# Second feed-forward of a transformer layer: five even features first on one token half alone, with their partial sums kept in DRAM

## The chip, the cores and the metric

The kernel runs on one core of a Trainium2 chip. The metric is the device time of one execution in microseconds (us), as the median of several runs. The engines are named as in the profile: PE multiplies matrices (PEld is its loading of weights), DVE, ACT and POOL do elementwise work, SP issues DMA transfers.

## What is computed

One layer works on 1024 latent tokens (a context of 256 tokens takes part in the mixing) with model width 1024 and feed-forward width 2816. The change lies in the second feed-forward alone, in the last line of this cut:

```python
def swiglu(h, w1, w3, w2):
    return (jax.nn.silu(h @ w1) * (h @ w3)) @ w2
...
x = x + 0.5 * m_l[2][:, None, :] * swiglu(modulate(rms_norm(x, norm1_w[i]), m_l[0], m_l[1]), ...)
y_l, y_c = token_mixing(modulate(rms_norm(x, norm2_w[i]), m_l[3], m_l[4]), ...)
x = x + m_l[5][:, None, :] * y_l
x = x + 0.5 * m_l[8][:, None, :] * swiglu(modulate(rms_norm(x, norm3_w[i]), m_l[6], m_l[7]), ...)
```

All of it is float32. m_l are nine modulation vectors, computed from c by a matrix product with ada_w.

## The kernel before, in words

**Precision.** A float32 operand is split into a high and a low part (`split`: ACT writes hi, DVE writes lo = x - hi). A product of two such operands is three matmuls, hi·hi, hi·lo, lo·hi (`mm3`, L424 to L428; the names hh and hl are the parts of h, whi and wlo those of a weight). One block product here is a block of 512 model rows by one feature block of 128 by 512 tokens: four k blocks of three matmuls, so 12 matmuls of 512 columns.

**The feed-forward in blocks.** The 2816 features are 22 blocks of 128 ("features" 0 to 21), taken in pairs (f, f+1); the tokens are two halves of 512 (0 and 1); the model rows are two halves. The product of a pair of features with both token halves is a 2 by 2 by 2 block product, which `chain` does with seven block products in place of eight (Winograd's form), from sums of weights (`seven_w`) and sums of h, called T1 to T4. A pair so has 7 products for w1 and 7 for w3, 168 matmuls. The result of w1 goes through silu on ACT (`c_silu`, L738), that of w3 is multiplied on DVE (`c_mul`, L743). When the four blocks g of a pair are there, `g_out` forms four differences on DVE (L751) and stores seven blocks to the DRAM tensor gd (L752), from which the last product with w2 reads them later.

**The opening.** T1 to T4 need the normed h of both halves, and the norm of half 1 is made only while PE has started. Therefore `first2` does features 0 and 1 without the seven-product form, on half 0 first (192 matmuls), while DVE and ACT finish the norm of half 1: `norm_t` makes for each of its k blocks nt (the scaled x), hh, hl and the raw sums of T1 and T2 (tiles t2h, t2l, t3h), all told at L147, since they come from the recorded steps of the mixing phase before. In that norm PE does two groups of eight small matmuls, psb<-ones,nacc and psb<-ndiag,ones. `HELD` puts the second of them behind a chosen matmul of the first product. Then `hidden` runs the pairs from 2 on: chain for w1, the sums of w2 (`w2_sums`, three loads by L792), chain for w3, and now and then a step of a modulation vector (L537, L538).

**What sets the order.** Every engine runs its instructions in the order in which the scheduler put them and stands still at one whose inputs are not ready. This is also so for SP, which issues all these transfers: a load behind a store that waits for DVE is issued after it. Loads of weights and their splits are pulled ahead by a priority (`WPRI`). Buffers: 6 raw weight tiles (`NR`), 6 split weights (`NH`), 19 tiles s of 128 by 512 (`ns`).

## Time and profile before

| | |
|---|---|
| median of 3 runs | 2084.39 us (2083.61 to 2087.27) |
| the profiled execution | 2088.82 us, of which the span 2087.0 us |
| PE clock granted, mean | 0.998 |
| PE busy | 2071.6 us (99% of the span) |
| DVE busy | 1471.9 us (71%) |
| ACT busy | 973.3 us (47%) |
| first product of the second feed-forward | starts at 1432.81 us |

The profile has a page and answers to queries of the trace. A row of the timeline reads: start, duration of one or of the whole group, engine, line, operation, output <- inputs, shape, and in brackets how long the engine had been idle and who released it. Rows of the waits read: engine and line that waited, for whom, us in total, times, longest. A row of windows has the stretch, then for each engine busy time and count, the PE clock granted, the share of the DMA engines in use and GB/s. A DMA row ends with its size and the us from issue to landing. Matmuls are pipelined, so that the time of one is read from the distance of starts.

### The profile page before, as it was taken

What the parts mean: (1) busy time and instruction counts of PE and PEld (TensorE: products, weight loads), DVE (VectorE), ACT (ScalarE), POOL (GpSimd) and SP (SyncE); (2) the same over time, 40 slices, a digit from 0 to 9 for tenths busy, and PEclk for the clock granted to TensorE, in tenths of its full rate; (3) what the DMA queues carried; (4) which work ended last, traced back from release to release, by engine and by line L of the source; (5) the groups of instructions that cost most, each with busy time, mean ns of one, the idle gap of its engine ahead of it and who ended that gap; (6) DMA issues with size and microseconds to landing.
All of it is one profiled execution on the core that took longest, in us unless ns stands there. A gap on an engine that the chain in (4) does not pass through costs nothing.

```text
span 2087.0 us, 34162 instructions
## 1 busy us (share of the span) xinstructions
PE 2071.6 (99%) x12352; PEld 1763.0 (84%) x12352; DVE 1471.9 (71%) x2660; ACT 973.3 (47%) x1818; POOL 199.3 (10%) x195
## 2 busy tenths in 40 slices
PE   9999999999999999999999999999999999999998
PEld 6888888888889999998788988888888888888888
DVE  6889999666776445765577478767776666765586
ACT  5433433435544445566475246444434344344553
POOL 0000000000015665001021001000000000010000
PEclk9999999999999999999999999999999999999999
DMA  9277667449886553674233233242344444477774
GB/s 348 84 241 237 232 217 256 149 165 371 277 289 222 181 183 115 195 219 129 76 108 98 79 91 105 90 162 81 112 156 147 144 163 157 151 235 229 218 237 151
DMA packets 201082, 370.58 MB, mean 178 GB/s; under 512 B 23249, under 2 KB 35921, under 8 KB 200785
## 3 DMA queue, kind: packets, MB, share of 16 engines
q1 hardware_dynamic: 200768, 368.33, 53.7%
q8 instruction: 97, 1.59, 0.3%
q14 instruction: 73, 0.59, 0.1%
q10 hardware_dynamic: 144, 0.07, 0.0%
HBM read 292.68 MB, written 67.24 MB: 172 GB/s over the span
## 4 chain that ended last, share of the span: by engine, by line
PE 77%; DVE 10%; DMA 8%; issue 3%; ACT 1%; SPq 0%; DVEq 0%; POOLq 0%; ACTq 0%
PE psa L147 18%; PE psa L426 10%; PE psa L428 10%; PE psa L427 10%; PE psb L147 9%; PE psb L427 7%; PE psb L428 7%; PE psb L426 7%; DVE junk L523 2%; DVE wlo L422 2%; DMA raw<-in_w 2%; DMA raw<-sd 2%; DVE hl L422 1%; DMA raw<-gd 1%; DMA hl<-sd 1%
## 5 line engine op out<-in xcount | busy, mean ns | idle before, releaser
L421 ACT ACTIVATE whi<-raw 128x512 fp32r<-128x512 f32 x371 | 233.9, 631 | 502.7 <-issue 160.6
L422 DVE TENSOR_TENSOR wlo<-raw,whi 128x512 fp32r<-128x512 f32 x371 | 254.1, 687 | 178.0 <-ACT whi L421 175.6
L426 PE MATMUL psa<-hh,whi 128*128 128x512 f32 x684 | 267.0, 390 | 1.2 <-ACT s L738 0.6
L428 PE MATMUL psa<-hh,wlo 128*128 128x512 f32 x684 | 266.3, 389 | 0.0
L427 PE MATMUL psa<-hl,whi 128*128 128x512 f32 x684 | 266.2, 389 | 0.0
L427 PE MATMUL psb<-hl,whi 128*128 128x512 f32 x568 | 221.6, 390 | 0.5 <-DVE hl L422 0.3
L428 PE MATMUL psb<-hh,wlo 128*128 128x512 f32 x568 | 221.3, 390 | 0.2 <-DVE wlo L422 0.2
L426 PE MATMUL psb<-hh,whi 128*128 128x512 f32 x568 | 221.1, 389 | 0.0
L426 PEld LDWEIGHTS psa<-hh,whi 128*128 128x128 f32 x684 | 128.4, 188 | 28.9 <-ACT s L711 1.7
L147 DVE TENSOR_TENSOR wlo<-raw,whi 128x512 fp32r<-128x512 f32 (+1 forms) x140 | 88.5, 647 | 90.8 <-ACT whi L147 80.1
L147 PE MATMUL psa<-hl,whi 128*128 128x512 f32 x384 | 152.5, 397 | 0.0
L147 PE MATMUL psa<-hh,whi 128*128 128x512 f32 x384 | 152.3, 397 | 0.0
L147 PE MATMUL psa<-hh,wlo 128*128 128x512 f32 x384 | 152.2, 396 | 0.0
L428 PEld LDWEIGHTS psa<-hh,wlo 128*128 128x128 f32 x684 | 128.4, 188 | 26.6
L427 PEld LDWEIGHTS psa<-hl,whi 128*128 128x128 f32 x684 | 128.5, 188 | 26.3
L422 POOL TENSOR_TENSOR hl<-s,hh 128x512 fp32r<-128x512 f32 x88 | 132.4, 1530 | 145.2 <-DVE hl L422 81.1
L147 ACT ACTIVATE whi<-raw 128x512 fp32r<-128x512 f32 (+1 forms) x140 | 82.5, 599 | 119.7 <-PE psa L147 94.1
L427 PEld LDWEIGHTS psb<-hl,whi 128*128 128x128 f32 x568 | 106.6, 188 | 24.7 <-DVE hl L422 2.7
L428 PEld LDWEIGHTS psb<-hh,wlo 128*128 128x128 f32 x568 | 106.6, 188 | 23.1 <-DVE wlo L422 1.2
L426 PEld LDWEIGHTS psb<-hh,whi 128*128 128x128 f32 x568 | 106.6, 188 | 22.2
L428 PE MATMUL psa<-hh,hl 128*128 128x256 f32 x392 | 111.1, 284 | 0.0
L426 PE MATMUL psa<-hh,hh 128*128 128x256 f32 x392 | 111.1, 283 | 0.0
(443 smaller groups left out, 4820.4 us busy)
## 6 DMA issues: line engine op xcount, KB each, us to landing
raw<-in_w SPq DMA_DIRECT2D x242, 256.0 KB, 3.3
s<-in_w SPq DMA_DIRECT2D x198, 256.0 KB, 3.7
gd<-s SPq DMA_DIRECT2D x154, 256.0 KB, 2.8
ada<-in_adaT SPq DMA_DIRECT2D x60, 512.0 KB, 4.6
raw<-gd SPq DMA_DIRECT2D x91, 256.0 KB, 3.5
sd<-s SPq DMA_DIRECT2D x44, 256.0 KB, 2.7
raw<-sd SPq DMA_DIRECT2D x44, 256.0 KB, 3.2
hh<-in_w SPq DMA_DIRECT2D x44, 256.0 KB, 4.0
```

Source lines behind the costliest of these rows:

```text
L147: self.rec.add(self.eng, lambda: f(*map(get, a), **{x: get(v) for x, v in k.items()}), outs, ins, name, a, k)
L421: nc.scalar.activation(hi, src, AF.Copy)
L422: (eng or nc.vector).tensor_tensor(out=lo, in0=src, in1=hi.bitcast(F32), op=ALU.subtract)
L426: mm(ps, wa[0], xa[0], start=start, stop=False, skip_group_check=more)
L427: mm(ps, wa[0], xa[1], start=False, stop=False, skip_group_check=more)
L428: return mm(ps, wa[1], xa[0], start=False, stop=stop, skip_group_check=more)
L523: nc.vector.tensor_tensor_reduce(out=self.junk, in0=t, in1=self.cs[s], scale=1.0, scalar=self.col("ada_b")[:, j:j + 1], op0=ALU.mult, op1= ...
```

## The change

The features 0, 2, 4, 6 and 8 are now treated in two steps.

`part(f)` takes the place of `first2`. It works on feature f and token half 0 alone. For w1 and w3 it does the first block product (12 matmuls each) into a PSUM bank; ACT copies the bank to a tile (L750), and a DMA stores the tile to a new DRAM tensor c1d (L751). Then the second product is added in the same bank, which finishes feature f on half 0: silu, multiplication, and a store of that g to gd (L755). This is 48 matmuls for each of the five parts. The splits of T1 and T2 stand between the parts 2 and 4, the raw sums of T3 and T4 between the parts 6 and 8, and their splits behind part 8.

`hidden(0, ..., 10)` then takes all pairs. The pairs 0 to 8 go through `rest`: of the seven products of each weight, the first (the saved one) and the second (feature f on half 0) are left out, which leaves five (W6, W5, W7, W3, W4), 120 matmuls for the pair. The saved sum is loaded from c1d (L776), copied by ACT into the bank (L794), and W6 accumulates on it. For w3 the saved g is loaded from gd as well (L779), and `g_out` doesn't store it again. The pairs 10 to 20 go through `chain` as before. The norm of half 1 makes no hh and hl for its first four k blocks, and the number HELD is 3 in place of 6.

```diff
 def norm_t ...
-            t = self.norm_k(tg, k, a, b, rb, pool)
+            t = self.scr(pool, "nt")
+            self.norm_a1(tg, k, a, rb, t)
...
+    def part(self, f):
+        ws = [self.load_halves(w[f]) for w in (self.w1, self.w3)]
+        ps = self.psA(), self.psB()
+        mms = []
+        for i in range(2):
+            for k in range(4):
+                mms.append(self.mm3(ps[i], self.wslice(ws[i], k), self.h[0][k], k == 0, k == 3))
+            t = self.stile()
+            self.nc.scalar.copy(t, ps[i])
+            self.nc.sync.dma_start(self.c1d[i, f // 2], t)
+        for i in range(2):
+            self.prod4(ws[i][1], self.h[0][4:], ps[i], False)
+            (self.c_mul if i else self.c_silu)(f, 0, ps[i], True)
+        self.nc.sync.dma_start(self.gd[1, f // 2], self.g[f, 0])
+        self.g[f, 0] = None
+        return mms
...
+    def rest(self, w, f, out, bank):
+        nc, i = self.nc, int(w is self.w3)
+        with self.tc.high_priority(offset=WPRI):
+            c1 = self.stile()
+            nc.sync.dma_start(c1, self.c1d[i, f // 2])
+            if i:
+                self.g[f, 0] = self.stile()
+                nc.sync.dma_start(self.g[f, 0], self.gd[1, f // 2])
+                self.again.add(f)
+            w6, w5, w7, w3, w4 = self.five_w(w, f)
...
+        a, b = bank(), bank()
+        nc.scalar.copy(a, c1)
+        self.prod4(w6, t2, a, False)
+        u2 = keep(a)
+        self.prod4(w5, t1, b, True)
+        c5 = keep(b)
+        self.prod4(w7, t3, a, False)
+        u3 = keep(a)
+        out(f + 1, 1, plus(c5, u3, c5))
+        self.prod4(w3, self.h[1][4:], b, False)
+        out(f, 1, plus(u2, b, u2))
+        self.prod4(w4, t4, a, False)
+        out(f + 1, 0, a, True)
...
-        put(1, b11), put(2, b21), put(3, b22)
+        if f not in self.again:
+            put(1, b11)
+        put(2, b21), put(3, b22)
...
-            self.chain(self.w1, f, self.c_silu, self.psA)
+            chain = self.rest if f < parts else self.chain
+            chain(self.w1, f, self.c_silu, self.psA)
...
+        mms = self.part(0)
+        tc.add_manual_dep(rec.diags[-4].ins, mms[HELD].ins.name, SCHED, reason="order")
+        self.part(2)
         for i, raw in enumerate((self.t1r, self.tr)):
             for k in range(4):
                 self.t_split(tp, i, k, raw[k])
-        raw = self.first2(tp, rec.diags[-4])
-        late = (None for _ in self.mods_half(f2, (8,)))
+        self.part(4)
+        self.part(6)
+        raw = [self.t34_raw(k) for k in range(4)]
+        self.part(8)
...
-        self.hidden(2, lambda: next(late, None))
+        late = (None for _ in self.mods_half(f2, (8,)))
+        self.hidden(0, lambda: next(late, None), False, 10)
...
-HELD = 6
+HELD = 3
```

Where the instructions now stand is shown at three places. Rows of the listing have the line, the operation and output <- inputs, with the number of each tile.

First place, ACT in the opening. The tiles t1h, t2h are hi parts of T1 and T2, hh_3173 is of the last k block of half 1, whi_15981 of a weight of part 4; psa_15785 and psb_15786 are the banks with the first products of part 0. Of the changed kernel:

```order
L422 ACTIVATE whi_15981<-raw_15979 128x512
L147 ACTIVATE hh_3173_15752<-nt_15748,mod_87 128x512
L422 ACTIVATE t1h_3243_15941<-t2l_3194_15750 128x512
L422 ACTIVATE t2h_3247_15949<-t3h_3096_15421 128x512
L422 ACTIVATE t2h_3251_15957<-t3h_3098_15458 128x512
L750 COPY s_15799<-psa_15785 128x512
L750 COPY s_15814<-psb_15786 128x512
```

The copies of part 0's first products stand behind the whole norm of half 1 and the hi parts of T1 and T2; by the listing of PE, 72 matmuls (the first products of the parts 0, 2 and 4) stand ahead of part 0's second product.

Second place, SP's queue between w3 of pair 2 and w1 of pair 4. The tiles s_16611 to s_16750 are blocks g of pair 2 and their differences, raw_17008 to raw_17012 weights of pair 6, s_16753 a piece for a modulation vector, s_16756 the saved sum for w1 of pair 4. Of the changed kernel:

```order
L665 DMA raw_17008<-in_w 128x512
L665 DMA raw_17010<-in_w 128x512
L823 DMA gd<-s_16611 128x512
L823 DMA gd<-s_16742 128x512
L823 DMA gd<-s_16745 128x512
L823 DMA gd<-s_16553 128x512
L823 DMA gd<-s_16750 128x512
L538 DMA s_16753<-in_adaT 128x512
L776 DMA s_16756<-c1d 128x512
L665 DMA raw_17012<-in_w 128x512
```

A seam between two pairs in the kernel before has these rows (s_16439 to s_16447 are blocks g and differences, the raw tiles weights that are used after a further weight set):

```order
L752 DMA gd<-s_16439 128x512
L752 DMA gd<-s_16281 128x512
L752 DMA gd<-s_16442 128x512
L752 DMA gd<-s_16222 128x512
L663 DMA raw_16770<-in_w 128x512
L752 DMA gd<-s_16447 128x512
L663 DMA raw_16772<-in_w 128x512
```

The load of the saved sum is new behind the pair's last stores; before, only loads of later weights stood there.

Third place, SP's queue between w1 and w3 of pair 4 of the changed kernel (raw_17133 is a weight of w3 of pair 6, s_16869 to s_16871 are blocks of w2, s_16879 is the saved sum for w3 of pair 4, s_16881 the saved g):

```order
L665 DMA raw_17133<-in_w 128x512
L538 DMA s_16866<-in_adaT 128x512
L865 DMA s_16869<-in_w 128x512
L865 DMA s_16870<-in_w 128x512
L865 DMA s_16871<-in_w 128x512
L776 DMA s_16879<-c1d 128x512
L779 DMA s_16881<-gd 128x512
```

Here the saved sum stands behind a weight load, a load for the modulation and the three loads of w2.

More of the change, by code (lines that the diff above doesn't have):

```diff
@@ L404, in __init__ @@
         self.sds = [self.nc.dram_tensor(f"sd{i}", (2, NP, P, 512), F32, kind="Internal").ap() for i in range(2)]
+        self.c1d = self.nc.dram_tensor("c1d", (2, NP, P, 512), F32, kind="Internal").ap()
         for n, s in (("cgk", (256, CTX)), ("crk", (512, CTX)), ("cgv", (CTX, 512)), ("crv", (CTX, 512)), ("p89d", (P, CTX)), ("s0g", (4, P, P)),
@@ L734, in chain, with prod4 @@
         out(f + 1, 0, a, True)
+    def prod4(self, wh, b, ps, start, stop=True):
+        for k in range(4):
+            self.mm3(ps, [t[:, k * P:(k + 1) * P] for t in wh], b[k], start and k == 0, k == 3, not start)
+    def part(self, f):
[3 more added lines that the diff above has]
+        for i in range(2):
+            for k in range(4):
+                mms.append(self.mm3(ps[i], self.wslice(ws[i], k), self.h[0][k], k == 0, k == 3))
[8 more added lines that the diff above has]
+        return mms
@@ new lines, in five_w @@
+    def five_w(self, w, f):
+        e = self.nc.vector
+        lo, hi = slice(0, 512), slice(512, 1024)
+        a11, a21, a22 = (self.raw_half(w[i][:, q]) for i, q in ((f, lo), (f + 1, lo), (f + 1, hi)))
+        s1 = self.raw_half()
+        a12 = self.raw_half(w[f][:, hi])
+        e.tensor_tensor(out=s1, in0=a21, in1=a22, op=ALU.add)
+        e.tensor_tensor(out=a21, in0=a11, in1=a21, op=ALU.subtract)
+        e.tensor_tensor(out=a11, in0=s1, in1=a11, op=ALU.subtract)
+        r = [self.half(a11), self.half(s1), self.half(a21)]
+        e.tensor_tensor(out=a12, in0=a12, in1=a11, op=ALU.subtract)
+        return r + [self.half(a12), self.half(a22)]
@@ new lines, in rest, with keep, plus @@
+    def rest(self, w, f, out, bank):
[8 more added lines that the diff above has]
+            w6, w5, w7, w3, w4 = self.five_w(w, f)
+        t1, t2, t3, t4 = self.T
+        def keep(ps):
+            t = self.stile()
+            nc.scalar.copy(t, ps)
+            return t
+        def plus(o, x, y):
+            nc.vector.tensor_tensor(out=o, in0=x, in1=y, op=ALU.add)
+            return o
+        a, b = bank(), bank()
[11 more added lines that the diff above has]
+        out(f + 1, 0, a, True)
@@ L814, in w2_tile, with hidden @@
         return a
-    def hidden(self, f0, mods=lambda: None, hold=False):
+    def hidden(self, f0, mods=lambda: None, hold=False, parts=0):
         for f in range(f0, NF, 2):
@@ L819, in hidden @@
                 self.held = []
-            self.chain(self.w1, f, self.c_silu, self.psA)
+            chain = self.rest if f < parts else self.chain
+            chain(self.w1, f, self.c_silu, self.psA)
             if f > f0:
                 mods()
-            self.w2_sums(f // 2 - 1)
-            self.chain(self.w3, f, self.c_mul, self.psB)
+            if f:
+                self.w2_sums(f // 2 - 1)
+            chain(self.w3, f, self.c_mul, self.psB)
             if f > f0:
@@ L967, in ffn_open @@
         self.w1, self.w3, self.w2 = (self.I[f"w{i}{j}"] for j in (1, 3, 2))
-        self.gates_m, self.fp, self.s, self.g = gates, pool, {}, {}
+        self.gates_m, self.fp, self.s, self.g, self.again = gates, pool, {}, {}, set()
         self.gd, self.sd = self.gds[i - 1], self.sds[i - 1]
@@ L1143, in t_make @@
         yield
-    def first2(self, tp, diag):
-        t3 = [self.tile(tp, [P, 512], F32R, f"t3l{k}") for k in range(4)]
-        t3 = [tuple(t3[2 * i:2 * i + 2]) for i in range(2)]
-        ws = {}
-        for f in range(2):
-            for i, w in ((0, self.w1), (1, self.w3)):
-                ws[f, i] = self.load_halves(w[f], t3 if (f, i) == (1, 1) else (None, None))
-        raw = []
-        for tg in LATTG:
-            for f in range(2):
-                ps = self.psA()
-                mms = self.proj(ws[f, 0], tg, ps)
-                if tg == f == 0:
-                    self.tc.add_manual_dep(diag.ins, mms[HELD].ins.name, SCHED, reason="order")
-                self.c_silu(f, tg, ps, True)
-                if tg:
-                    raw.append(self.t34_raw(2 * f))
-                self.c_mul(f, tg, self.H(ws[f, 1], tg))
-                if tg:
-                    raw.append(self.t34_raw(2 * f + 1))
-        return raw
     def first1(self, pools, n1):
```

## The prediction

> **What bounds the kernel now.** I read the profile page first, then the windows of the second feed-forward, then TensorE's (PE's) waits in it, then the timeline of its opening and of a seam between two pairs.

> ```profile
> PE 2071.6 (99%) x12352; PEld 1763.0 (84%) x12352; DVE 1471.9 (71%) x2660; ACT 973.3 (47%) x1818; POOL 199.3 (10%) x195
> PE 77%; DVE 10%; DMA 8%; issue 3%; ACT 1%; SPq 0%; DVEq 0%; POOLq 0%; ACTq 0%
> 1500.00:1600.00 100.00, 100.00 (x443) 82.81 (x442) 67.98 (x110) 38.38 (x67) 0.00 (x0) 1.00 0.45 155
> PE psa L426 <- ACT s L738: 0.6, 1, 0.6
> PE psb L427 <- DVE hl L422: 0.3, 1, 0.3
> ```

> PE is busy 99% of the span and holds 77% of the chain that ended last. In the window 1500 to 1600 us it runs 443 matmuls without a gap at the full clock (1.00), so one costs 100/443 = 0.226 us; I use 0.227, the distance of two starts in the timeline. A row's 0.39 us is longer because matmuls overlap. The last two rows are all the waits of PE from 1430 to 1960 us. So this stage is pure matmul time: removing matmuls pays in full, and any new wait costs in full, for no slack is left to take it.

> **The change, part by part.** The result is a small gain in matmuls and a set of new waits.

> *Removed.* For features 0 to 9 there were 192 matmuls of the classical product and 4 pairs of 168, 864 together. Now there are five parts of 48 and five pairs of 120, 840 together; the pairs from 10 on stay as they are. That is 24 matmuls fewer, 24 x 0.227 = **-5.4 us**. The wait of 0.6 on L738 goes too (PE's loss there, read between starts, is 0.8): **-0.8**.

> *The opening.* These rows are of before, where first2 covers the norm of token half 1:

> ```profile
> 1432.81 0.39 PE L426 MATMUL psa<-hh,whi 128*128 128x512 f32 x1
> 1438.75 1.16 PE L147 MATMUL psb<-ndiag,ones 128*128 128x128 f32 x8
> 1440.56 1.41 DVE L147 SCALAR_TENSOR_TENSOR nt<-x,mod,nrb 128x512 f32<-128x512 f32 x2 [1.28 <-ACT nrb L147]
> 1455.57 0.74 DVE L147 SCALAR_TENSOR_TENSOR t3h<-nt,mod,t2l 128x512 f32<-128x512 f32 x1
> 1456.35 0.63 ACT L421 ACTIVATE t2h<-t3h 128x512 fp32r<-128x512 f32 x1 [1.34 <-DVE t3h L147]
> 1456.88 0.58 ACT L738 ACTIVATE s<-psa 128x512 f32<-128x512 f32 x1
> ```

> DVE works on that norm from 1440.56 to 1456.31: 24 instructions, 0.655 each. ACT takes its instructions in order, so a silu of a product that was done near 1440 comes only at 1456.88. The change puts the copies of the partial sums (L750) in the same place, behind the last t2h. By the listing DVE now has 27 instructions from the first nt to the last t3h: four hl fewer, but weight splits and t1l are now among them. 27 x 0.655 from 1440.56 ends at 1458.2; t2h (0.63) and the copy (0.58) end at 1459.5. PE has only first products to run meanwhile: 72 matmuls from 1432.81 are 16.3 us, the norm's two groups of eight small matmuls cost about 1 each (the ndiag row has 1.16 with its tail), and with ndiag now behind 12 matmuls instead of 18, PE stands 1.1 before it. It comes to the first second product at 1452.2 and waits until 1459.5: **+7.3**, and **+1.1**. Later the copies of part 8 stand in ACT behind hi copies of T3 and T4 that wait for DVE's raw sums: about **+3.5**, from the same pitches; the first pair's start another **+0.6**. These two are my least certain terms; from nothing to double is 0 to 8.

> *The seams.* A rest pair begins each weight with ACT's copy of c1 into the bank (L794), and W6 accumulates on it. So PE waits for load, then copy. In what row of SP's queue the load stands decides everything, for SP issues in order and stands still at each wait. Rows of before:

> ```profile
> 1555.87 3.34 SPq L752 DMA_DIRECT2D gd<-s  x4
> 1559.27 0.42 SPq L537 DMA_DIRECT2D s<-in_adaT  x1
> 1559.99 0.68 DVE L751 TENSOR_TENSOR s<-s,s 128x512 f32<-128x512 f32 x1
> 1560.70 0.32 SPq L752 DMA_DIRECT2D gd<-s  x1
> 1561.11 0.38 SPq L663 DMA_DIRECT2D raw<-in_w  x1
> 1480.89 1.89 DVE L751 TENSOR_TENSOR s<-s,s 128x512 f32<-128x512 f32 x3
> 1482.15 0.63 ACT L421 ACTIVATE whi<-raw 128x512 fp32r<-128x512 f32 x1 [3.78 <-PE psa L427]
> 1482.69 0.57 ACT L711 COPY s<-psa 128x512 f32<-128x512 f32 x1
> ```

> The last store of g is issued at 1560.70, right where DVE's L751 ends (1560.67), and the weight load at 1561.11 only behind it: the queue does stand. Before, nothing behind it was needed for tens of us.

> From w3 to the next pair's w1, take 0 as the moment at which PE could go on. By the listing c1's load stands behind the pair's g stores and one load for the modulation. The last store needs: whi of the next W6 (it waits for the eleventh matmul of the last product, about 0; 0.63), its wlo, two multiplications and four subtractions on DVE (seven at 0.605, from the row of three in 1.89, with 0.08 of tail): 0.67 + 4.3 = 5.0. Then the store's issue 0.33, the load's 0.42: c1 is issued at 5.8. Landing and copy follow:

> ```profile
> raw<-in_w SPq DMA_DIRECT2D x1, 256.0 KB, 3.3
> s<-in_adaT SPq DMA_DIRECT2D x1, 256.0 KB, 2.9
> s<-in_w SPq DMA_DIRECT2D x1, 256.0 KB, 3.8
> s<-in_w SPq DMA_DIRECT2D x1, 256.0 KB, 4.9
> 1536.19 1.37 SPq L792 DMA_DIRECT2D s<-in_w  x3
> ```

> Loads nearly alone took 2.9 and 3.3; I take 3.0. The copy is 0.58, the hand-overs 0.05 each, and one hoisted matmul is taken off: PE waits 9.3. Into pairs 4, 6 and 8 that is **+27.9**. Into pair 2 only three stores and no modulation load stand ahead: **+7.5**.

> From w1 to w3 of a pair, c1's load stands behind a weight load that waits for the wlo of the previous weight set's last half; DVE does that wlo behind a sum that waits for w1's fourth product, one product (2.7) before the seam. Sum 0.61 and wlo 0.69 with the matmul's tail 0.17 make 1.55, then issues of the weight load, the modulation load and three loads of w2 (0.41 + 0.46 + 1.4): c1 is issued 3.8 after the fourth product. It is the sixth of a burst in which the third to fifth landed after 3.8 to 4.9; I take 5.1. With copy and hand-overs 9.6, less 2.7 and the hoisted 0.23: 6.7. Pairs 2, 4 and 6: **+20.1**. Pair 0 has shorter queues, **+2.3**; at pair 8 21 matmuls of pair 10 are pulled ahead and only a weight split is late, **+1.9**.

> No row of before shows a load of c1. The nearest bounds are 2.9 (alone) and 4.9 (burst) at all eight. With 2.9 everywhere the seams sum to 51, with 4.9 everywhere to 67; my 59.7 lies between, and I keep both ends for the range.

> Sum of waits: 1.1 + 7.3 + 3.5 + 0.6 + 27.9 + 7.5 + 20.1 + 2.3 + 1.9 = 72.2, less 6.2 = **+66**.

> [...]

> *The clock.* PE will now stand still for 7 to 9 us at a time. The trace has one such place:

> ```profile
> 1021.80:1025.30 3.50, 1.66 (x97) 1.35 (x97) 2.30 (x10) 1.83 (x5) 0.00 (x0) 1.00 0.26 80
> 1025.30:1028.80 3.50, 3.50 (x44) 2.39 (x46) 1.97 (x7) 0.70 (x2) 0.00 (x0) 0.51 0.02 5
> 1026.03 0.63 PE L147 MATMUL psa<-hl,whi 128*128 128x512 f32 x1
> 1026.45 0.63 PE L147 MATMUL psa<-hh,wlo 128*128 128x512 f32 x1
> ```

> After 3.5 us with PE busy for 1.66, the next 3.5 us were granted 0.51 of the clock, and matmuls started 0.42 apart instead of 0.227. Half of such a stretch is lost, 1.7 us. Eight gaps are longer than 3.4 us (the opening, part 8's, three of 6.7, one of 7.5 and three of 9.3 make nine, the shortest doubtful): 8 x 1.7 = **+13.6**.

> [...]

> **The sum.** The profiled run took 2088.82 us, of which the span is 2087.0; the median of the runs is 2084.39, 4.4 below. The durations are of the profiled run, the differences I put on the median: 2084.4 + 66 + 13.6 = **2164**.

> **Rivals.** First, the loads of c1 are not late: other waits free SP earlier than the listing suggests. Then only ACT's order counts at a seam: whi, silu, copy, about 1.5 into w3 and 1.0 into w1, four of each, and 1.9. With the opening (12.5) less 6.2, and 1.7 twice for the clock, that is 2084.4 + 10 + 1.9 + 12.5 - 6.2 + 3.4 = **2106**. Against it: SP's row at 1560.70 waits for DVE exactly as I price it.

> Second, the clock stays full through the gaps: **2150**. For it: the only place in the trace that shows the drop has other, small matmuls around it.

> Third, on the other side: every copy finds its source ready. Its place is the copy L750 or L794 ahead of an accumulating product, its price nothing. It decides if c1 is issued over 3.6 us (3.0 and the copy) before the seam, and if DVE is through the norm by 1451, that is with about 16 instructions from 1440.56 instead of 27. Then only the 24 matmuls and the old wait count: 2084.4 - 6.2 = **2078**. The listing speaks against both conditions.

> Fourth, the change doesn't do what it says: the five products would have to be hidden in other matmuls. The listing has 24 matmuls fewer and no others, so I give this no chance of its own; and if it fails only in the waits it is one of the above.

> **How the numbers follow.** Forecast 0.62; full clock 0.17; loads in time 0.10; all hidden 0.04; above 2195, with landings of 5 us at every seam, 0.05; within 0.2% by halves of these, 0.02. 0.2% is about what a measurement of this kernel can tell from no change. The range starts from 2150, the sum without the clock. Downwards the seams give 9 and the two small terms of the opening 4: 2137. Upwards they give 7 and 4, and the clock 13.6, or twice that if two stretches follow each gap: 2188. Cases between the forecast and the two outer ones (loads in time at some seams only, landings of 5 us at some) I take in with another 11 below and 7 above: 2126 to 2195. That leaves out the loads in time and the faster case. Faster 0.04, within 0.2% 0.02, slower 0.94.

> **What would show it.** In the changed profile PE's waits should name ACT's copy L794 nine times or so, with 6 to 9 us each in pairs 2 to 8, and L750 once with some 7 us. The chain of waits should run there through a DMA of c1d and through SP's queue behind L823. Windows of 3.4 us behind a gap should show a clock near 0.5. I am wrong if L794 waits for ACT alone (rival one), if the clock in those windows is 1.00 (rival two), or if no row of PE's waits names L750 (rival three).

## The result and the profile after

The changed kernel takes **2181.34 us** (median of 4 runs, 2176.38 to 2184.35) against 2084.86 before: 1.0457 times as long, 95% interval 1.0437 to 1.0477. The forecast was 2164 in a range of 2126 to 2195. The profiled run took 2176.38 us with a span of 2174.6, 87.6 more than before.

The page of the changed kernel, its first part and its chain:

```profile
PE 2087.1 (96%) x12328; PEld 1769.2 (81%) x12328; DVE 1476.7 (68%) x2666; ACT 984.6 (45%) x1838; POOL 202.8 (9%) x195
PE 88%; issue 3%; DMA 3%; DVE 3%; ACT 1%; SPq 1%; POOL 0%; DVEq 0%; POOLq 0%; ACTq 0%
```

There are 24 matmuls fewer (12352 to 12328), yet PE's busy time is 15.5 us more: matmuls at half clock last longer (0.63 us a row behind the gap that ended at 1541.05, against 0.39 at full clock). The share of PE falls from 99% to 96%.

PE's waits from 1425 to 2050 us of the changed kernel (engine and line, for whom: us in total, times, longest):

```profile
PE psa L427 <- ACT psa L794: 38.1, 5, 10.1
PE psb L427 <- ACT psb L794: 24.4, 5, 7.5
PE psa L427 <- ACT s L750: 8.2, 2, 4.9
PE psa L427 <- ACT whi L422: 1.0, 2, 0.6
PE psb L147 <- DVE ndiag L147: 0.6, 1, 0.6
PE psb L427 <- ACT whi L422: 0.5, 1, 0.5
PE psb L429 <- DVE wlo L423: 0.5, 1, 0.5
```

Where before there were two rows with 0.9 us together, now 73.3 us stand, 62.5 of them for ACT's copy of a saved sum into the bank. That ACT is named doesn't make ACT the cause. The chain of waits of the changed kernel through the two seams of pair 4 shows what ACT waited for (start, duration, what; "issue" is time for which no wait is shown, here DVE's low part of a weight):

```profile
1580.64 0.64 ACT whi L422
1581.34 0.57 issue
1581.91 1.28 DVE s L814 x2
1583.20 0.61 DVE s L822
1583.83 1.91 DVE s L822 x3
1585.76 0.32 SPq L823
1586.13 0.44 SPq L538
1586.62 3.56 DMA s<-c1d
1590.21 0.60 ACT psa L794
1590.85 0.79 PE psa L427
...
1604.11 0.69 DVE wlo L423
1604.81 0.33 SPq L665
1605.19 0.42 SPq L538
1605.67 0.42 SPq L865
1606.14 0.43 SPq L865
1606.61 0.43 SPq L865
1607.09 5.60 DMA s<-c1d
1612.71 0.60 ACT psb L794
1613.35 0.79 PE psb L427
```

From w3 to w1 (the upper rows) the last g store, the modulation load and then the saved sum leave SP one after the other, and only 3.56 us later does ACT copy. PE could have gone on at 1580.85, so the load was issued 5.8 later, as forecast, and PE waited 10.0 (forecast 9.3). From w1 to w3 (the lower rows) the load leaves behind a weight load, a modulation load and three loads of w2, and takes 5.60 to land.

The clock behind another gap and in the middle of the first one above, by windows (stretch, length, busy time and count of PE, PEld, DVE, ACT and POOL, then TensorE's granted clock, DMA share, GB/s):

```profile
1541.10:1544.50 3.40, 3.40 (x8) 2.72 (x9) 0.00 (x0) 0.00 (x0) 0.00 (x0) 0.50 0.01 2
1544.50:1547.90 3.40, 3.40 (x13) 2.68 (x13) 0.69 (x1) 1.11 (x2) 0.00 (x0) 0.79 0.00 0
1583.40:1586.80 3.40, 0.00 (x0) 0.00 (x0) 2.29 (x4) 0.00 (x0) 0.00 (x0) 0.52 0.95 358
```

At full clock, with 0.227 from start to start, 15 matmuls start in 3.40 us. In the two windows behind the gap that ended at 1541.05 only 7 and 12 start (the rows count one more, which reaches over the edge): by the distances of the starts PE has lost 2.4 us there. The third row lies in the middle of the gap before 1590.85: the clock falls to a half while PE still stands.

### The profile page after: what moved, and what is told of

It is laid out like the page before. It is cut to its first block, busy times and chain, and to the rows that moved or that the text cites. A ratio compares the mean times of both kernels' runs of the same rounds, so it can differ in the third digit from the quotient of the medians.

```text
span 2174.6 us, 34258 instructions
## 1 busy us (share of the span) xinstructions
PE 2087.1 (96%) x12328; PEld 1769.2 (81%) x12328; DVE 1476.7 (68%) x2666; ACT 984.6 (45%) x1838; POOL 202.8 (9%) x195
## 4 chain that ended last, share of the span: by engine, by line
PE 88%; issue 3%; DMA 3%; DVE 3%; ACT 1%; SPq 1%; POOL 0%; DVEq 0%; POOLq 0%; ACTq 0%
PE psa L147 16%; PE psa L427 12%; PE psa L428 12%; PE psa L429 12%; PE psb L427 9%; PE psb L428 9%; PE psb L429 9%; PE psb L147 7%; DMA s<-c1d 2%; PE psa L1257 1%; DVE wlo L423 1%; DVE s L822 0%; PE psb L1257 0%; ACT whi L422 0%; DMA ada<-in_adaN 0%
## 5 line engine op out<-in xcount | busy, mean ns | idle before, releaser
L422 ACT ACTIVATE whi<-raw 128x512 fp32r<-128x512 f32 x379 | 239.1, 632 | 523.7 <-PE psb L428 143.1
L423 DVE TENSOR_TENSOR wlo<-raw,whi 128x512 fp32r<-128x512 f32 x379 | 260.3, 689 | 249.1 <-ACT whi L422 247.1
L427 PE MATMUL psa<-hh,whi 128*128 128x512 f32 x652 | 255.8, 392 | 9.8 <-ACT s L750 8.2
L428 PE MATMUL psa<-hl,whi 128*128 128x512 f32 x652 | 254.8, 391 | 0.0
L429 PE MATMUL psa<-hh,wlo 128*128 128x512 f32 x652 | 254.8, 391 | 0.0
L429 PE MATMUL psb<-hh,wlo 128*128 128x512 f32 x584 | 227.8, 390 | 0.7 <-DVE wlo L423 0.5
L427 PE MATMUL psb<-hh,whi 128*128 128x512 f32 x584 | 227.4, 389 | 0.5 <-ACT whi L422 0.5
L428 PE MATMUL psb<-hl,whi 128*128 128x512 f32 x584 | 227.6, 390 | 0.1
L427 PEld LDWEIGHTS psa<-hh,whi 128*128 128x128 f32 x652 | 123.2, 189 | 37.2 <-ACT s L750 9.1
L147 PE MATMUL psa<-hl,whi 128*128 128x512 f32 x384 | 151.9, 396 | 0.0
L147 PE MATMUL psa<-hh,wlo 128*128 128x512 f32 x384 | 151.9, 396 | 0.0
L147 PE MATMUL psa<-hh,whi 128*128 128x512 f32 x384 | 151.9, 396 | 0.0
L147 DVE TENSOR_TENSOR wlo<-raw,whi 128x512 fp32r<-128x512 f32 (+1 forms) x140 | 88.6, 649 | 91.8 <-ACT whi L147 81.0
L423 POOL TENSOR_TENSOR hl<-s,hh 128x512 fp32r<-128x512 f32 x88 | 131.5, 1520 | 145.9 <-DMA hl<-sd 81.9
L429 PEld LDWEIGHTS psa<-hh,wlo 128*128 128x128 f32 x652 | 123.0, 189 | 26.0 <-DVE wlo L423 0.4
L428 PEld LDWEIGHTS psa<-hl,whi 128*128 128x128 f32 x652 | 123.1, 189 | 25.2
L147 ACT ACTIVATE whi<-raw 128x512 fp32r<-128x512 f32 (+1 forms) x140 | 82.5, 600 | 119.3 <-PE psa L147 93.5
L429 PEld LDWEIGHTS psb<-hh,wlo 128*128 128x128 f32 x584 | 109.6, 188 | 24.8 <-DVE wlo L423 2.3
L427 PEld LDWEIGHTS psb<-hh,whi 128*128 128x128 f32 x584 | 109.6, 188 | 23.7 <-ACT whi L422 1.0
L427 PE MATMUL psa<-hh,hh 128*128 128x256 f32 x392 | 111.1, 283 | 0.0
## 6 DMA issues: line engine op xcount, KB each, us to landing
raw<-in_w SPq DMA_DIRECT2D x262, 256.0 KB, 3.1
s<-in_w SPq DMA_DIRECT2D x198, 256.0 KB, 3.8
gd<-s SPq DMA_DIRECT2D x154, 256.0 KB, 2.6
raw<-gd SPq DMA_DIRECT2D x91, 256.0 KB, 3.4
sd<-s SPq DMA_DIRECT2D x44, 256.0 KB, 2.9
raw<-sd SPq DMA_DIRECT2D x44, 256.0 KB, 3.0
hh<-in_w SPq DMA_DIRECT2D x44, 256.0 KB, 4.0
```

Of the source, the lines that this page charges most:

```text
L147: self.rec.add(self.eng, lambda: f(*map(get, a), **{x: get(v) for x, v in k.items()}), outs, ins, name, a, k)
L422: nc.scalar.activation(hi, src, AF.Copy)
L423: (eng or nc.vector).tensor_tensor(out=lo, in0=src, in1=hi.bitcast(F32), op=ALU.subtract)
L427: mm(ps, wa[0], xa[0], start=start, stop=False, skip_group_check=more)
L428: mm(ps, wa[0], xa[1], start=False, stop=False, skip_group_check=more)
L429: return mm(ps, wa[1], xa[0], start=False, stop=stop, skip_group_check=more)
```

## The experiments

All times are medians. The runs of before beside them had medians of 2085.16 (first four experiments), 2085.79 (the next four) and 2085.99 (the last two).

**1. The loads of the saved sums on another queue.**

```diff
-            nc.sync.dma_start(c1, self.c1d[i, f // 2])
+            nc.gpsimd.dma_start(c1, self.c1d[i, f // 2])
```

> The loads of the saved sums go to POOL's DMA queue, so that no store of g, weight load or w2 load stands ahead of them. Queue theory (PE's wait at a seam is the late issue of this load): the 62.5 us that PE waits for L794 fall to 10 or less (ACT's order alone, 1.0 to 1.5 per seam), the half-clock stretches behind the seams go too, and the time falls from 2181 to about 2112. Copy theory (the wait is ACT's copy into the bank and its place in ACT's order, whenever the load lands): waits stay above 50, time within 10 of 2181.

2120.39 us (ratio 1.0164, 1.0149 to 1.0179): 61 of the 96 us are gone with this one word. PE's waits for the copy:

```profile
PE psb L427 <- ACT psb L794: 10.3, 4, 4.4
PE psa L427 <- ACT psa L794: 3.6, 5, 0.8
```

They fell from 62.5 to 13.9, so the queue theory holds and the copy theory falls. The time is 8 above the 2112 expected, and the waits are above the 10. From w3 to w1 the wait is now 0.8, ACT's order alone. From w1 to w3 of the pairs 4 and 6 it is still up to 4.4. The rows of SP, DVE and ACT ahead of that seam in pair 4 show another in-order wait behind it:

```profile
1570.62 6.43 SPq L665 DMA_DIRECT2D raw<-in_w  x3
1576.61 0.69 DVE L767 TENSOR_TENSOR raw<-raw,raw 128x512 f32<-128x512 f32 x1
1577.41 0.63 ACT L422 ACTIVATE whi<-raw 128x512 fp32r<-128x512 f32 x1 [0.65 <-DVE raw L767]
1577.95 0.58 ACT L809 ACTIVATE s<-psa 128x512 f32<-128x512 f32 x1
1578.43 0.59 ACT L794 COPY psb<-s 128x512 f32<-128x512 f32 x1
```

The saved sum had been issued at 1570.28 and took 3.0 us, so it lay there by 1573.3. But ACT's copy stands behind the hi part of the next weight, whose sum on DVE came late, behind weight loads that SP issues only as buffers come free (6.43 us for the three of the first row).

**2. The loads of the saved sums left out.** ACT copies a tile that is in SBUF anyway.

```diff
-            c1 = self.stile()
-            nc.sync.dma_start(c1, self.c1d[i, f // 2])
+            c1 = self.T[0][0][0].bitcast(F32)
```

> The loads of the saved sums are left out; ACT copies a tile that lies in SBUF anyway into the bank, so the five products of a rest pair add to wrong numbers. Copies and order else stay. Queue theory: as with the load on a free queue, about 2112, with L794 waits of 10 or less; what is left is ACT's order. Copy theory: 2181 as before. If the ten loads' traffic itself mattered, this one would be below the one with the loads on POOL's queue by more than 5.

2091.57 us (1.0028, 1.0016 to 1.0039). No wait for L794 is left at all, and the time is 20 below what I expected. My expectation took ACT's order as fixed. In the listing of this kernel the copies stand up to several instructions earlier, ahead of the previous weight's last copies, since a copy that waits for no load is placed earlier. So the price of ACT's order in the forecast's first rival depends on the load being there. Between this kernel and the one with the loads on POOL's queue lie 29 us in the medians and 24 in the profiled spans. All waits of PE from 1425 to 2050 us add up to 8.2 us here and to 25.8 there (13.9 of them for L794, and 2.4 more than here at the copies L750), and the half clock costs 4.5 and 7.0 by the granted clock of the two traces (0.997 and 0.995 in the mean). That is 20 of the 24; the rest is open. By the last sentence of the expectation such a difference would speak for the traffic of the ten loads, but the order changed too, so this run alone can't tell. Experiment 6 can: it keeps the ten loads and takes 2093.61 us.

**3. Only the g stores moved away.**

```diff
-        store = lambda i, t: nc.sync.dma_start(self.gd[i, f // 2], t)
+        store = lambda i, t: (nc.gpsimd if f in self.again else nc.sync).dma_start(self.gd[i, f // 2], t)
```

> Only the stores of g and its differences for the rest pairs go to POOL's queue; the load of the saved sum stays on SP. Queue theory: from w3 to w1 the load then stands behind a weight load that waits for the wlo of W6 (1.4 after the seam) and a modulation load, so it is issued at about 2.3 instead of 5.8: three waits of 10 become about 6.7 and that of pair 2 loses 2 to 3; the four from w1 to w3 stay near 7.4. Sum of L794 waits 62.5 - 13 = 49, time about 2168. Copy theory: no change, 2181.

2169.71 us (1.0402, 1.0386 to 1.0417), close to the expected 2168. PE's waits and SP's rows at the seam into pair 4:

```profile
PE psa L427 <- ACT psa L794: 26.6, 5, 7.3
PE psb L427 <- ACT psb L794: 24.8, 5, 7.8
```

```profile
1578.59 2.75 SPq L665 DMA_DIRECT2D raw<-in_w  x2
1581.40 0.42 SPq L538 DMA_DIRECT2D s<-in_adaT  x1
1581.91 0.38 SPq L776 DMA_DIRECT2D s<-c1d  x1
```

Only the waits on psa, from w3 to w1, became shorter (38.1 to 26.6); those on psb stayed (24.4 and 24.8). So the stores are what held the load at the one kind of seam, and not at the other. At the seam shown, PE could have gone on at 1579.84. The load, now behind a weight load that waits for DVE, leaves 2.1 us after that instead of 5.8, takes 4.64 to land instead of 3.56, and the copy takes 0.60: that is why some 7 us remain.

**4. The gaps filled with unused matmuls.**

```diff
         a, b = bank(), bank()
+        for n in range(FILL.get((f, i), 0)):
+            mm = nc.tensor.matmul(a, t1[0][0][:, :P], t1[0][0], start=True, stop=True)
+            if not n:
+                self.tc.add_manual_dep(mm.ins, self.last[1].ins.name, SCHED, reason="order")
         nc.scalar.copy(a, c1)
```

FILL has 26 to 34 for seven seams; W5 is held behind W6, as in the changed kernel.

> In seven seams 26 to 34 matmuls that nothing uses (208 in all, 47 us at full clock) are put where PE would stand still; they write into the bank ahead of ACT's copy, and are fewer than fit into the wait. Clock theory (about 2.1 us per seam are lost since PE comes back at half clock): granted clock near 1.00 behind the seams, time about 15 lower, 2166. If the lost time behind the seams is something else (weights late, ACT behind), the time stays at 2181 or above. The seams themselves stay as long in both.

2168.01 us (1.0386, 1.0367 to 1.0406), 13 less than the changed kernel with 208 matmuls more; between the two profiled runs it is 16 (2176.38 and 2160.08). The window 1530 to 1690 of the changed kernel and of this one:

```profile
1530.00:1690.00 160.00, 100.80 (x380) 80.07 (x379) 71.78 (x119) 38.13 (x66) 0.00 (x0) 0.80 0.39 133
```

```profile
1530.00:1690.00 160.00, 149.76 (x643) 120.80 (x643) 77.03 (x126) 43.84 (x76) 0.00 (x0) 0.99 0.41 141
```

The granted clock goes from 0.80 to 0.99. The seams stay as long; what PE still waits there (the copy's line is L800 in this kernel) is

```profile
PE psa L427 <- ACT psa L800: 8.4, 5, 2.3
PE psb L427 <- ACT psb L800: 4.8, 4, 2.9
```

and with 208 x 0.227 = 47.2 of filling that makes 60.4, against 62.5. So the half clock behind the seams is a cost of its own, of about 2 us per seam.

**5. The copies of the opening in tiles apart.**

```diff
-            t = self.stile()
+            t = self.tile(self.hp, [P, 512], F32R, f"h{'hl'[i]}1{f // 2}").bitcast(F32) if f < 8 else self.stile()
```

> In the opening the copies of the parts 0 to 6 go to tiles that nothing else uses yet, not to tiles s, whose memory the norm of half 1 still holds; in ACT's order they then stand among the norm's instructions instead of behind them. Theory: the wait of 5.1 at the first second product and the half clock behind it (1.8) go, 2181 - 7 = 2174. Rival: PE only comes earlier to part 8, whose copies stand behind the hi copies of T3 and T4, and waits there instead (3.5 now, then up to 9): 2181 or little below.

2169.07 us (1.0404, 1.0383 to 1.0424), 12 less in the medians and 9 in the profiled spans, where 7 were expected; the four runs lie up to 11 apart. PE's wait for the copies L750 in this kernel:

```profile
PE psa L427 <- ACT s L750: 3.3, 1, 3.3
```

The wait of 4.9 at the first second product is gone, that of 3.3 at part 8 is neither gone nor longer; the rival falls. In ACT's timeline the copies of part 0 stand at 1434.75 and 1440.44, where they stood at 1457.14 and 1457.61 behind the norm. Only the tiles that they write to were changed, so it was the memory of the tiles s that put the copies behind the norm. That the norm itself still holds this memory is my reading of the kernel, and no run tests it apart.

**6. The saved sum added afterwards.**

```diff
-        nc.scalar.copy(a, c1)
-        self.prod4(w6, t2, a, False)
+        self.prod4(w6, t2, a, True)
...
+        u3 = plus(u3, u3, c1)
...
+        u2 = plus(u2, u2, c1)
...
-        out(f + 1, 0, a, True)
+        out(f + 1, 0, plus(c1, a, c1))
```

> The load of the saved sum stays on SP where it was, but nothing is copied into the bank: W6 starts a fresh sum, and DVE adds the saved sum afterwards in SBUF (three more instructions of 0.6 per weight, 30 in all). Theory: PE waits for nothing of c1 any more; the 62.5 of L794 and the half clock behind the seams (about 17) go: about 2102, and at most 2110. Rival: DVE takes its instructions in order and stands still for c1, so that the low parts of the next weights come late and PE waits for L423 instead, 3 to 5 per seam: 2120 to 2140.

2093.61 us (1.0038, 1.0024 to 1.0051), with the loads in their late places on SP:

```profile
PE psa L427 <- ACT s L750: 4.9, 1, 4.9
PE psb L427 <- ACT s L786: 2.0, 2, 1.9
```

No wait for a saved sum is left, and the rival (DVE stands still in its turn) shows in one wait of 1.9. It is 8 below the expectation. Part 8's wait of 3.3 went as well: in PE's timeline W6 and W5 of pair 0, free of the saved sum now, stand ahead of part 8's second products, from 1491.75 to 1497.20, and give its copies time. And the expectation starts from the changed kernel's median, which lies 5 above its profiled run.

**7. Four parts instead of five.**

```diff
-        self.hidden(0, lambda: next(late, None), False, 10)
+        self.hidden(0, lambda: next(late, None), False, 8)
```

and part(8) left out, with the raw sums of T3 and T4 ahead of part(6).

> Features 0, 2, 4 and 6 alone (pair 8 goes through the seven products as the later ones); the count of matmuls is the same 24 fewer. Theory (cost per seam): the seams of pair 8 (10.2 and 0.5), its half clock (about 2.2 each for it and for one of part 8) and part 8's wait of 3.5 go: 2181 - 18 = 2163. Rival (a cost paid once, at the opening, or by the whole stage): less than 8 of change, above 2173.

2154.79 us (1.0332, 1.0316 to 1.0347): 26.5 less by the medians, 21 by the spans (2153.4). Its waits for the copies:

```profile
PE psa L427 <- ACT psa L794: 28.3, 4, 10.1
PE psb L427 <- ACT psb L794: 16.9, 3, 7.4
PE psa L427 <- ACT s L750: 8.2, 2, 4.9
```

Against the changed kernel, psa has lost 9.8 and psb 7.5, and L750 nothing: 17.3, and 2.0 of half clock for each of the two gaps make 21.3. So the cost is paid per pair, as the theory has it, but I had named the wrong two gaps: the last part keeps its wait of L750, whichever it is, and the last rest pair has a covered seam, because matmuls of the next pair are pulled ahead there.

**8 to 10. All mended.** Copies apart (5), sums afterwards (6), and in experiment 8 the loads on POOL's queue (1) and four parts (7); 9 has the loads on SP again, 10 five parts.

> Four parts, copies in tiles apart, loads of the saved sums on POOL's queue, sums added by DVE afterwards. If all waits found are all that the change costs, the 24 matmuls fewer and the old wait show: 2085 - 6 = 2079, and with some 3 left in the opening 2082. Rival: the opening cannot be covered by four parts, and what is won is lost there: 2086 to 2092.

> As the mended version, but the loads of the saved sums stay on SP in their late places. If taking the sum off PE's path is enough, the time is that of the mended version, 2082 within 2; if DVE's order makes up for the late load (its sums stand before the low parts of the next weights), it is 4 or more above.

> As the mended version, but with five parts as in the change. Theory: a part and its rest pair cost nothing once their waits are gone, and the count of matmuls is the same, so 2082 within 2; if part 8's copies behind the hi copies of T3 and T4 still hold PE, 3.5 and some 2 of half clock more, 2087.

Experiment 8 takes 2082.11 us (0.9981, 0.9973 to 0.9990), 9 takes 2082.86 (0.9985, 0.9975 to 0.9995), 10 takes 2081.34 (0.9977, 0.9966 to 0.9987). All three are a little faster than before and don't differ from each other beyond their intervals, so taking the sum off PE's path is enough, and the rival of 9 falls; in the profile of 9 PE still waits 1.5 us for L786. All that PE waits for from 1425 to 2050 us in experiment 8, and the window 1432 to 1850 in it:

```profile
PE psb L147 <- DVE ndiag L147: 0.6, 1, 0.6
```

```profile
1432.00:1850.00 418.00, 417.27 (x1845) 344.03 (x1844) 314.75 (x518) 178.52 (x312) 6.11 (x10) 1.00 0.50 167
```

Its span is 2080.9, 6.1 below that of before; the removal of 24 matmuls and of the old wait was worked out as 6.2. That the two agree so closely is partly luck. From the first product to the last one on T3 the stage takes 421.7 us before (1432.81 to 1854.55) and 417.2 here (1432.31 to 1849.53), 4.5 less, and the medians show 3.7. So the change's arithmetic is a small gain, and its loss is in the waits and the half clock behind them.

## Why the prediction was right, step by step

- **Removed, -6.2.** Right in kind, and a little too large: experiment 8 shows 4.5 in the stage, where 5.6 were due with its new wait of 0.6 for ndiag, and 3.7 in the medians.
- **w3 to w1, 27.9 and 7.5, and 0.6 for the first pair: 36.0.** Measured 38.1 (psa). The path was the one forecast, to the single instruction, and the issue came at 5.8 as worked out. The landing took 3.56 where I took 3.0 from lone loads. The first pair waited 0.4.
- **w1 to w3, 20.1 and 2.3: 22.4,** and 1.9 at pair 8 for a weight split. Measured 24.4 (psb), and 2.0 in the three rows of whi and wlo, though two of these stand in the opening. I took a landing of 5.1; it was 5.60.
- **The opening, 7.3 and 1.1; part 8, 3.5.** Measured 8.2 for both waits of L750 (4.9 and 3.3), and 0.6. The first of them is 2.4 shorter than forecast. PE came later than I had it, since it also waited 0.5 twice for a weight's hi and lo part there, and DVE was through the norm a little sooner. The reason that I gave for the place of the copies, ACT's order, was only half of it: the order itself followed from the memory of the tiles (experiment 5).
- **The sum of waits, 72.2.** Measured 73.3. The errors of the terms are up to 2.4 and cancel, so that it is luck that the sum fits this well. A row counts a wait from the modelled end of the last matmul, 0.39 after its start, though the next could have started 0.227 after it; read between starts the waits are 76.3.
- **The clock, 13.6.** This is the mis-sized term. 87.6 of span, plus 6.2 for what was removed, less 73.3 leaves 20.5, but some 2 to 3 of that are the waits as read between starts. By the distances of the matmuls' starts behind the gaps, the clock cost 18.1. I took half of one stretch of 3.4 us, 1.7, for eight gaps longer than 3.4. That a gap has to be that long is shown by no run: 2.7 us in experiment 3 brought a clock of 0.50, and 2.6 us in the changed kernel left it at 1.00. All nine gaps above 3.3 us had it, with 1.4 to 2.7 each, 2.0 in the mean, since the lower clock often reaches into a second window, as in the rows above. The rival with a full clock falls by these rows and by experiment 4.
- **From the span to the median.** I set the differences on the median of before, 4.4 below its profiled run. The profiled run after was the lowest of its four, 5.0 below their median. So the medians are 96.5 apart where the profiled runs are 87.6 apart. These 9 us are not in any term of the sum: the other three runs show a granted clock of 0.978 or 0.979, the profiled one 0.982, which suggests more time at half clock in them, but they have no trace and this stays open. Of the 17 us between the forecast and the result, then, some 5 are the clock, some 4 the waits read between starts, and the rest is this step.

The rivals: the loads of c1 were late (experiment 1 shows what the first rival would have looked like, at 2120 instead of 2106, with a new wait behind the weight loads); the copies didn't find their sources ready, and the version in which they do is 2082, not 2078.

## What to carry to other kernels

A transfer that PE waits for belongs on a queue in which nothing that waits stands ahead of it, or off PE's path altogether (PE's waits for the copy fell from 62.5 us to 13.9 in experiment 1, and none was left in experiment 6); look for it in the order of the issuing engine, since the profile names the engine that passes the data on. This stage, with PE at 100% from 1500 to 1600 us before, had no slack, so that a saving forecast at 6.2 us was lost many times over to the late loads of the saved sums, 62.5 us of waits. A gap of PE of 3.3 to 10.1 us cost its length here and 1.4 to 2.7 us more for the clock.

## What I had not expected of the hardware

```profile
1515.24:1518.65 3.41, 2.07 (x10) 1.38 (x8) 2.30 (x4) 1.50 (x3) 0.00 (x0) 1.00 0.56 169
1518.65:1522.06 3.41, 2.28 (x10) 1.87 (x11) 0.00 (x0) 0.59 (x1) 0.00 (x0) 1.00 0.43 138
```

```profile
1517.84:1521.25 3.41, 0.91 (x4) 0.45 (x4) 0.94 (x2) 1.56 (x3) 0.00 (x0) 1.00 0.84 293
1521.25:1524.66 3.41, 3.41 (x9) 2.63 (x9) 0.00 (x0) 0.00 (x0) 0.00 (x0) 0.50 0.03 13
```

In the changed kernel the gap is shared by two steps, and PE is busy for 2.07 and 2.28 us of them; in experiment 3 nearly all of it lies in one, with 0.91 us busy, and the next step has half the clock. From 1440 to 2040 us of the changed kernel the clock fell behind nine steps, in each of which PE was busy for 1.35 us or less, and stayed full behind all the others, the least busy of which had 2.07. It came back behind steps with 2.83 us or more, and stayed low behind steps with up to 2.21: the gap that ended at 1541.05 ended in a step with 1.49 us busy, and the next step had 0.50 as well. In the kernel before, the clock fell at 1025.37 behind a step with 1.58 us busy, among smaller matmuls. That it was the busy time of a step that counted, so that the place of a gap in the steps was luck, is my reading of these figures; no run tests it apart.
